# Four quadrants for the inverse's levels, and whole triangular blocks in seven transfers a half

## The chip, the core and the metric

The kernel runs on one core of one Trainium2 chip, in one launch. The metric is device time in microseconds of that core. TensorE (PE in the profile) does the matmuls and the transposes, VectorE (DVE) and ScalarE (ACT) the elementwise work, GpSimd (POOL) a few memsets, and the queue of SyncE (SP) issues every transfer, in the order in which the program has them. Each engine works through its own instructions in program order and waits where an operand is not there yet.

## The reference

One block of a hybrid model over 256 latent and 256 context tokens of width 2048: a modulated RMSNorm, one wide input projection, a bidirectional RWKV-7 branch of 16 heads, a latent-attention branch of 8 heads, gates, and an output projection. What the change touches is the recurrence of the RWKV branch, which runs over the context first and then over the latent tokens, in both directions `d`:

```python
def rwkv7_step(S, xs):
    r, w, k, v, kk, akk = xs
    sa = jnp.einsum("dbhij,dbhj->dbhi", S, -kk)
    S = S * w[..., None, :] + sa[..., :, None] * akk[..., None, :] + v[..., :, None] * k[..., None, :]
    return S, jnp.einsum("dbhij,dbhj->dbhi", S, r)
```

The kernel computes it in chunks of 64 tokens. Inside a chunk the terms `sa` depend on each other through a triangular 64x64 matrix A, so each chunk needs the inverse of a unit triangular matrix made from A.

## The kernel before, in words

All data are float32. Large products are done in three passes of split operands (`mm3`: high·high, high·low, low·high); each piece of weights `w` is loaded by SP, split into `wh` (ACT) and `wl` (DVE), and multiplied into an accumulator `acc`. Small products are plain float32 matmuls, and the profile has two records for each of these.

**Stages.** The norm, the modulation and the first projection take the start (to about 135 us). The RWKV stage follows (about 135 to 890 us): the 16 heads are 8 pairs, two heads of 64 channels on the two halves of the 128 partitions, and a pair has a context half (256 tokens) and a latent half, so there are 16 halves. Then come the attention branch and the merging products.

**The RWKV stage.** It is written as generators, which `drive` takes forward by an estimated clock. `front_chain` prepares halves (decays, keys, the triangular matrices `AQ`); `back_chain` takes groups: group 0 is the first pair's context half alone, groups 1 to 7 are the latent half of one pair beside the context half of the next, group 8 is the last latent half alone; `lanes` holds one generator `diagonal` for each half, one after the other; and where none of them is due, the planner puts in projection work (`bg`). The planner's waits in `diagonal` are the five numbers `LT`. They set only the order of the program, not a time on the chip. Each engine's instructions thus have a fixed order.

**The inverse of one half.** A half has 8 chunks-and-directions `u`, and 2 heads `g`, so 16 triangular 64x64 blocks. `diagonal` inverts the four 16x16 blocks on each diagonal: it writes them to DRAM (`dl`, 8 transfers), reads them back so that each of the 64 blocks of a `g`, `b` and `u` has a partition (`ln`, 1), inverts them by 28 small DVE steps and a few copies (`wt`, blocks and their transposes), writes them out (`dw`, 1), and reads them into the diagonal of `WT` (8), a tile of zeros otherwise: 18 transfers. There are two `WT`, one for context halves and one for latent halves; a new half is read into one once the `levels` of the group before are done.

**The levels.** `back` then finishes the inverses of a group in four steps, each with 16 matmuls of 64x64 by 64x64 for each half: first `Z` = the mask `zoff` times (`AQ`, `WT`), and then three times `W` = `WT` + (`Z` times `W`), where the first has `WT` in place of `W`. `lev` does one half's 16 matmuls: head 0 reads partitions 0 to 63 and writes PSUM partitions 0 to 63, head 1 reads 64 to 127 and writes 64 to 127. One DVE operation of 128x512 follows for each half (the mask, or the add of `WT`). After the levels the group goes through its four chunks (`chp` matmuls with `UV`, `xs`, `W`, `BKT`, `AR`, `QR`).

**The context half's products.** In `front` a context half's `AQ` comes from 8 matmuls of 128x128 by 128x128 with the block-diagonal tile `Qbd` (two heads, zeros between them); a latent half's from `QR`, by head, from 64 partitions each, in a burst (`E.burst`: after the first matmuls the rest of the group gets a high priority and is put behind them, so that nothing comes between).

In the profile, nearly all DVE and ACT instructions have the line of a helper (L141), and matmuls that of `Tensor.matmul` (L114, L116, L119); the names of the tiles tell them apart.

Of the kernel before, what the change touches and what calls it, by code (L numbers as in the profile page):

```python
# [16 lines left out]
P = 128  # L17
# [13 lines left out]
_CW = [("ident", 128), ("ones", 128), ("mq", 128), ("mr", 128),  # L31
# [29 lines left out]
LT = (3.0, 3.0, 2.0, 3.0, 4.0)  # L61
# [84 lines left out]
def hybrid_block(  # L146
# [128 lines left out]
    with tc.tile_pool(name="p1", bufs=2) as p1:  # L275
        xT = p1.tile([P, KT, TT], F32, name="xT", bufs=1)
# [47 lines left out]
        for k in range(KT):  # L324
# [6 lines left out]
            E.matmul(pst[32 * g:32 * g + 32], lhsT=con("ones")[:, 0:32], rhs=sq, start=k < 4, stop=k >= KT - 4,  # L331
# [4 lines left out]
        for i in range(4):  # L336
            E.matmul(pst[:, 2 * i:2 * i + 2], lhsT=sqs[:, 128 * i:128 * i + 128], rhs=con("ones")[:, 0:2], start=True, stop=True)
# [9 lines left out]
        E.matmul(pst, lhsT=con("ones"), rhs=dg.rearrange("p i t -> p (i t)"), start=True, stop=True)  # L347
# [244 lines left out]
    with tc.tile_pool(name="rw", bufs=1) as rw:  # L592
        WTs = []
        for i in range(2):
            WTs.append(rw.tile([P, 2, NU, CH], F32, name=f"WT{i}"))
            nc.gpsimd.memset(WTs[i], 0.0)


        Qbd = rw.tile([P, 2, 4, 2, CH], F32, name="Qbd")
        nc.gpsimd.memset(Qbd, 0.0)  # L600
# [10 lines left out]
        hss = [slice(0, 64), slice(64, 128)]  # L611
# [80 lines left out]
        def front(h, k, mi, rho):  # L692
# [67 lines left out]
            Q = rw.tile([P, 2, 4, 2, CH], F32, name="QR", bufs=2) if lat else Qbd  # L760
            ex = [slice(0, 64), slice(1, 65)]
            kkc = kk[:, ts].rearrange("p (c t) -> p c t", t=CH)
            for d in range(2):
                if lat:
                    V.scalar_tensor_tensor(Q[:, d, :, 0], kkc, -1.0, Ep3[d][:, :, ex[d]], ALU.mult, ALU.mult)
                else:
# [33 lines left out]
            else:  # L800
                for d in range(2):
                    ps = wk()
                    pv = ps.rearrange("p (c g t) -> p c g t", c=4, g=2)
                    for c in range(4):
                        E.matmul(pv[:, c], lhsT=BK[:, 4 * d + c].rearrange("p a t -> p (a t)"), rhs=Q[:, d, c], start=True, stop=True)
# [110 lines left out]
        def back(hs_, UV, rho):  # L916
# [695 lines left out]
```

## Time and profile before

| | |
|---|---|
| Time of 3 runs | 1264.83, 1268.13, 1276.66 us; median 1268.13 |
| The profiled execution's own time | 1267.55 us, of which its span is 1265.7 us |
| Granted TensorE clock, mean | 0.995 |
| Busy over the span | PE 1208.8, weight loads 1023.7, DVE 953.7, ACT 577.6, POOL 3.3 us |
| The RWKV stage, 200 to 890 us | PE 662.64, DVE 572.66, ACT 293.85 us busy of 690; DMA engines 0.42 |
| Matmuls of the levels (`lv`, 200 to 890 us) | 2048 records, PE 74.83 us |
| Transfers of a half's inverse | `dl` 8 of 8 KB, `ln` 64 KB, `dw` 128 KB, `WT` 8 of 16 KB |

A row of a timeline is: start, length, engine, line, operation, out<-in, shapes, count, and in brackets the idle time before it and what ended it. Matmuls overlap, and the length of one is its way through the array, so the pace of a sequence is read from the distances of the starts and not from the lengths. "x128" of the levels is 64 matmuls.

### The profile page before, as it was taken

Reading aid. Unit: us, or ns where it says so; the run is one execution under the profiler, and the core shown is the slowest. Engines: PE = TensorE matmul, PEld = TensorE weight load, DVE = VectorE, ACT = ScalarE, POOL = GpSimd, SP = SyncE. Lnnn points to the kernel's source line nnn. Section 1 sums busy time; section 2 is a strip of 40 time slices with the busy share of each in tenths; the row PEclk is TensorE's granted clock in tenths of the full one; section 3 lists DMA queues with packets and bytes.
Section 4 is the critical chain, followed back from the end, with each engine's and each line's share of the span. In section 5 each row is a group of like instructions: output and inputs, shape, how many; then the busy total and the mean of one; then the engine's idle time right before and its main releaser. Section 6 shows DMA issues by size and latency. Waiting matters only on the chain. (4 is left out here: it accounts for less than half of the span.)

```text
span 1265.7 us, 30073 instructions
## 1 busy us (share of the span) xinstructions
PE 1208.8 (96%) x11485; PEld 1023.7 (81%) x11485; DVE 953.7 (75%) x2658; ACT 577.6 (46%) x1216; POOL 3.3 (0%) x9
## 2 busy tenths in 40 slices
PE   6999999998999989999989999999999999899998
PEld 2566878787887877878778789889899999899886
DVE  4444777877898878888878988875876777768655
ACT  3444543442543434524524344444465656545443
POOL 0000000000000000000000000000000000000000
PEclk9999999999999999999999999999999999999999
DMA  9999345443442433443534345334765433589674
GB/s 377 347 358 335 130 146 165 145 125 115 125 131 78 135 91 106 138 113 92 152 98 118 107 132 155 108 102 136 249 197 159 131 115 115 185 275 304 217 256 140
DMA packets 170288, 212.10 MB, mean 168 GB/s; under 512 B 66512, under 2 KB 94816, under 8 KB 169632
## 3 DMA queue, kind: packets, MB, share of 16 engines
q1 hardware_dynamic: 170144, 210.18, 52.8%
q8 instruction: 90, 1.47, 0.5%
q14 instruction: 54, 0.44, 0.1%
HBM read 195.30 MB, written 14.82 MB: 166 GB/s over the span
## 5 line engine op out<-in xcount | busy, mean ns | idle before, releaser
L141 ACT CAST wh<-w 128x512 fp32r<-128x512 f32 (+1 forms) x484 | 290.9, 607 | 349.1 <-PE acc L119 142.8
L141 DVE TENSOR_TENSOR wl<-w,wh 128x512 fp32r<-128x512 f32 (+1 forms) x480 | 322.4, 674 | 144.8 <-ACT wh L141 73.7
L119 PE MATMUL acc<-hmh,wl 128*128 128x256 f32 (+1 forms) x1312 | 396.8, 302 | 5.2 <-DVE wl L141 4.5
L119 PE MATMUL acc<-hml,wh 128*128 128x256 f32 (+1 forms) x1312 | 393.5, 300 | 0.0
L119 PE MATMUL acc<-hmh,wh 128*128 128x256 f32 (+1 forms) x928 | 273.1, 294 | 0.0
L119 PEld LDWEIGHTS acc<-hmh,wl 128*128 128x128 f32 x1312 | 247.6, 189 | 20.6 <-DVE wl L141 9.2
L119 PEld LDWEIGHTS acc<-hml,wh 128*128 128x128 f32 x1312 | 248.2, 189 | 9.3 <-issue 1.0
L119 PEld LDWEIGHTS acc<-hmh,wh 128*128 128x128 f32 x928 | 175.4, 189 | 5.0
L116 PE MATMUL acc<-hmh,wh 128*128 128x256 f32 (+1 forms) x384 | 144.6, 377 | 6.5 <-DVE th L141 3.9
L116 PEld LDWEIGHTS acc<-hmh,wh 128*128 128x128 f32 x384 | 72.4, 189 | 32.0 <-issue 13.0
L141 DVE TENSOR_TENSOR pr<-wt 64x14 f32<-64x14 f32 (+6 forms) x224 | 42.7, 191 | 3.4
L141 DVE TENSOR_TENSOR wt<-wt,pr 64x14 f32<-64x14 f32 (+6 forms) x224 | 42.4, 189 | 3.3
L114 PE MATMUL a<-hmh,wh 128*128 128x512 f32 x96 | 40.7, 424 | 0.0
L114 PE MATMUL pm<-wm,ssil 128*32 128x256 f32 x512 | 35.0, 394 | 5.0 <-DMA wm<-in_w_mod_ss 4.9
L141 DVE TENSOR_TENSOR W<-WT,lv 128x512 f32<-128x512 f32 x48 | 32.2, 684 | 9.5 <-PE lv L114 9.5
L114 PE MATMUL a<-hmh,wl 128*128 128x512 f32 x96 | 38.0, 396 | 0.0
L114 PE MATMUL a<-hml,wh 128*128 128x512 f32 x96 | 37.9, 394 | 0.0
L114 PE MATMUL lv<-W,Z 64*64 64x64 f32 x1024 | 33.8, 220 | 3.9 <-DVE W L141 3.9
L114 PEld LDWEIGHTS lv<-W,Z 64*64 64x64 f32 x1024 | 31.7, 135 | 5.9 <-DVE W L141 5.1
L114 PE MATMUL chp<-obh,wh 128*128 128x256 f32 x128 | 36.2, 283 | 0.0
L114 PE MATMUL chp<-obh,wl 128*128 128x256 f32 x128 | 36.2, 283 | 0.0
L114 PE MATMUL chp<-obl,wh 128*128 128x256 f32 x128 | 36.2, 283 | 0.0
(327 smaller groups left out, 2166.3 us busy)
## 6 DMA issues: line engine op xcount, KB each, us to landing
w<-in_w_proj SPq DMA_DIRECT2D x296, 256.0 KB, 2.9
wm<-in_w_mod_ss SPq DMA_DIRECT2D x64, 512.0 KB, 7.2
w<-in_w_mod_g SPq DMA_DIRECT2D x64, 256.0 KB, 3.1
w<-in_w_br SPq DMA_DIRECT2D x64, 256.0 KB, 3.9
w<-in_w_out SPq DMA_DIRECT2D x64, 256.0 KB, 3.5
w<-in_w_first SPq DMA_DIRECT2D x32, 192.0 KB, 4.8
thd<-th SPq DMA_DIRECT2D x48, 128.0 KB, 2.9
xT<-in_xcT SPq DMA_DIRECT2D x4, 1024.0 KB, 8.4
```

Of the source, the lines that this page charges most:

```text
L114: return self.engine.matmul(out, lhsT=lhsT, rhs=rhs, **kw)
L116: self.head.append(self.engine.matmul(out, lhsT=lhsT, rhs=rhs, **kw))
L119: i = self.engine.matmul(out, lhsT=lhsT, rhs=rhs, **kw)
L141: return fn(out, *a, **kw)
```

## The change

The levels of a group with two halves are put into one burst, in which the matmuls of the two halves alternate; the latent half (member 0) stays on its partitions, and the context half (member 1) writes each result to the other 64 partitions than those that it reads, so that the four combinations of input and output halves come in turn. For this, `TF` is a copy of the context half's `WT` blocks with the partition halves exchanged, and `ZN` such a copy of its `Z` (four ACT copies of 64x512 for a group). Of its four steps, the first writes crossed, the next writes back, and so on.

`diagonal` moves whole 64x64 blocks: `dl` takes all of `AQ` (2 transfers), `ln` picks the diagonal blocks on its way from DRAM (1), `dw` puts the inverses on the diagonals of DRAM blocks that were filled with zeros once at the start (2, one for blocks and one for transposes), and `WT` is read whole (2): 7 transfers. `dw` is now one tile for each kind of half that stays, where a rotating tile was. `LT` is changed. The context half's products use a plain `Q` tile (`Qc`) and 16 matmuls with 64 partitions each, in a burst, in place of the 8 with `Qbd`. The constant `ones` of 128 columns is replaced by 2 columns and a memset tile in the two places that need more; `xs` shares a buffer with `ZN`.

```diff
-LT = (3.0, 3.0, 2.0, 3.0, 4.0)
+LT = (3.5, 5.0, 2.0, 4.5, 5.5)
+PD = CH * CH + CH
...
-            nc.gpsimd.memset(WTs[i], 0.0)
...
-        nc.gpsimd.memset(Qbd, 0.0)
+        WTs = [rw.tile([P, 2, NU, CH], F32, name=f"WT{i}") for i in range(2)]
+        nc.gpsimd.memset(WTs[0], 0.0)
+        dws = [dr1.tile([2, 8, 2, PD], F32, name=f"dw{i}") for i in range(2)]
+        for t in dws:
+            rows = t.rearrange("w u g (b x) -> (w u g b) x", b=4)
+            zero = WTs[0].rearrange("p w u t -> p (w u t)")
+            nc.sync.dma_start(rows[:, 0:16 * CH], zero)
+            nc.sync.dma_start(rows[:, 16 * CH:PD // 4], zero[:, 0:PD // 4 - 16 * CH])
...
-                    for g in range(2):
-                        hs = hss[g]
-                        V.scalar_tensor_tensor(Q[hs, d, :, g], kkc[hs], -1.0, Ep3[d][hs, :, ex[d]], ALU.mult, ALU.mult)
+                V.scalar_tensor_tensor(Q[:, d, :, 0], kkc, -1.0, Ep3[d][:, :, ex[d]], ALU.mult, ALU.mult)
...
-                    for c in range(4):
-                        E.matmul(pv[:, c], lhsT=BK[:, 4 * d + c].rearrange("p a t -> p (a t)"), rhs=Q[:, d, c], start=True, stop=True)
+                pv = [v4(wk()) for _ in range(2)]
+                with E.burst(tc, 2):
+                    for d in range(2):
+                        for c in range(4):
+                            for g in (1, 0):
+                                E.matmul(pv[g][:, d, c], lhsT=BK[hss[g], 4 * d + c].rearrange("p a t -> p (a t)"),
+                                         rhs=Q[hss[g], d, c, 0], start=True, stop=True)
...
+        def blocks(t):
+
+            return t.rearrange("u g (b x) -> (u g b) x", b=4)[:, 0:16 * CH].rearrange("p (r c) -> p r c", c=CH)[:, :, 0:16]
+
+        def diagonal(group, AQ, WT, dw):
+
+            dl = dram.tile([8, 2, PD], F32, name="dl", tag="dl")
             for g in range(2):
...
+                nc.sync.dma_start(dl[:, g, 0:CH * CH].rearrange("u (r c) -> r u c", c=CH), AQ[hss[g], g])
...
+            nc.sync.dma_start(ln, blocks(dl))
...
+            for w in range(2):
+                nc.sync.dma_start(blocks(dw[w]), wt[:, w])
...
+                nc.sync.dma_start(WT[hss[g]].rearrange("p w u t -> p (w u) t"),
+                                  dw[:, :, g, 0:CH * CH].rearrange("w u (r c) -> r (w u) c", c=CH))
...
-            def lev(fn):
-                ps = lvp()
-                for u in range(8):
-                    for g in range(2):
-                        fn(ps[hss[g], 64 * u:64 * u + 64], hss[g], g, u)
-                return v4(ps)
+            def lev(fns, outs, heads=n):
+                ps = [lvp() for _ in fns]
+                with E.burst(tc, heads):
+                    for u in range(8):
+                        for g in range(2):
+                            for t, fn, out in zip(ps, fns, outs):
+                                fn(t[hss[g ^ out], 64 * u:64 * u + 64], g, u)
+                return [v4(t) for t in ps]
...
+            def crossed(dst, src):
+
+                for g in range(2):
+                    S.copy(dst[hss[1 - g]], src[hss[g]])
...
+            if n == 2:
+                TF = rw.tile([P, 512], F32, name="TF")
+                crossed(v4(TF), top(WTs[0]))
+            ps = lev([lambda o, g, u, AQ=t[3], WT=WTs[t[1]]: E.matmul(o, lhsT=AQ[hss[g], g, u], rhs=WT[hss[g], 1 - u // 4, u], start=True, stop=True)
+                      for t in mem], (0, 1), 2 * n)
...
+            if n == 2:
+                ZN = rw.tile([P, 512], F32, name="ZN", tag="zx")
+                crossed(ZN, Zs[1])
...
+                for m in range(n):
+                    x = m * (1 - i % 2)
+                    Z = ZN if m and i == 1 else Zs[m]
+                    W = Ws[m] if i else TF if m else None
+                    fns.append(lambda o, g, u, Z=Z, W=W, x=x, WT=WTs[mem[m][1]]: E.matmul(
+                        o, lhsT=blk(Z, hss[g ^ x], u), rhs=WT[hss[g], u // 4, u] if W is None else blk(W, hss[g ^ x], u), start=True, stop=True))
+                ps = lev(fns, (0, i % 2))
+                for m in range(n):
+                    V.tensor_tensor(u4(W2[:, m]), v4(TF) if m and i == 1 else top(WTs[mem[m][1]]), ps[m], ALU.add)
```

**PE, the levels of group 4, before.** `WT_1358` is the context half's tile, `Z` and `W` the tiles of the levels, `QR` and `UV` belong to other steps:

```order
L114 MATMUL lv<-WT_1358,AQ 64x64 x15
L114 MATMUL chp<-UV,AQ 64x64 x4
L116 MATMUL wk<-QR,BK 128x128 x2
L119 MATMUL wk<-QR,BK 128x128 x6
L114 MATMUL lv<-WT_1358,Z 64x64 x16
L114 MATMUL lv<-W_6808,Z 64x64 x64
```

The last two steps of both halves stand in one row of 64 matmuls, half after half.

The same place now, from the end of the second step to the head of the third (`WT_1361` is the latent half's tile):

```order
L120 MATMUL lv<-WT_1361,Z 64x64
L120 MATMUL lv<-TF,Z 64x64
L117 MATMUL wk<-QR,BK 128x128 x2
L120 MATMUL wk<-QR,BK 128x128 x6
L117 MATMUL lv<-W_6863,Z 64x64
L117 MATMUL lv<-W_6863,ZN 64x64
```

The halves alternate matmul by matmul inside a step, and between two steps stands a piece of other work, here 8 products with `QR`; between the third and the fourth step there is a burst of `acc`.

**SP, the end of the second half's `diagonal`, before.** `dw` and `WT` are the two last transfers of the inverse, `w` are weights:

```order
L899 DMA dw<-wt 64x2x256
L236 DMA w<-in_w_proj 128x512
L906 DMA WT_1360<-dw 16x16x16 x8
L236 DMA w<-in_w_proj 128x512 x3
L236 DMA w<-in_w_mod_g 128x512 x2
```

And now, for the third half:

```order
L237 DMA w<-in_w_proj 128x512
L901 DMA dw_1363<-wt 64x16x16 x2
L905 DMA WT_1360<-dw_1363 64x16x64 x2
L237 DMA w<-in_w_proj 128x512 x3
L237 DMA w<-in_w_mod_g 128x512 x2
```

Nine transfers are four, and here no weights stand between the write and the read.

**SP, the start of the RWKV stage.** Now, the zero fill of both `dw` stands behind the first two pieces of the projection, where before 12 pieces followed each other:

```order
L707 DMA th<-in_wup 128x256
L237 DMA w<-in_w_mod_g 128x512 x2
L237 DMA w<-in_w_proj 128x512 x2
L603 DMA dw_1363<-WT_1360 128x1024
L604 DMA dw_1363<-WT_1360 128x16
L603 DMA dw_1364<-WT_1360 128x1024
L604 DMA dw_1364<-WT_1360 128x16
L237 DMA w<-in_w_proj 128x512 x10
```

Four transfers have moved in ahead of ten pieces of weights, and they read the tile that POOL sets to zero.

More of the change, by code (lines that the diff above doesn't have):

```diff
@@ L28 @@
 QK_SCALE = 192.0 ** -0.5
-_CW = [("ident", 128), ("ones", 128), ("mq", 128), ("mr", 128),
+_CW = [("ident", 128), ("ones", 2), ("mq", 128), ("mr", 128),
        ("zoff", 128), ("bones", 128), ("hsel", 2),
@@ L275, in hybrid_block @@
     with tc.tile_pool(name="p1", bufs=2) as p1:
+        ones = p1.tile([P, P], F32, name="ones", bufs=1)
+        nc.gpsimd.memset(ones, 1.0)
         xT = p1.tile([P, KT, TT], F32, name="xT", bufs=1)
@@ L330, in hybrid_block @@
             g = k % 4
-            E.matmul(pst[32 * g:32 * g + 32], lhsT=con("ones")[:, 0:32], rhs=sq, start=k < 4, stop=k >= KT - 4,
+            E.matmul(pst[32 * g:32 * g + 32], lhsT=ones[:, 0:32], rhs=sq, start=k < 4, stop=k >= KT - 4,
                      tile_position=(0, 32 * g))
@@ L336, in hybrid_block @@
         for i in range(4):
-            E.matmul(pst[:, 2 * i:2 * i + 2], lhsT=sqs[:, 128 * i:128 * i + 128], rhs=con("ones")[:, 0:2], start=True, stop=True)
+            E.matmul(pst[:, 2 * i:2 * i + 2], lhsT=sqs[:, 128 * i:128 * i + 128], rhs=con("ones"), start=True, stop=True)
         mod_a(0)
@@ L346, in hybrid_block @@
         V.tensor_tensor(dg, ident.unsqueeze(1).to_broadcast([P, 4, P]), rms[:, 0:8:2].unsqueeze(2).to_broadcast([P, 4, P]), ALU.mult)
-        E.matmul(pst, lhsT=con("ones"), rhs=dg.rearrange("p i t -> p (i t)"), start=True, stop=True)
+        E.matmul(pst, lhsT=ones, rhs=dg.rearrange("p i t -> p (i t)"), start=True, stop=True)
         rsb = p1.tile([P, TT], F32, name="rsb", bufs=1)
@@ L592, in hybrid_block @@
     with tc.tile_pool(name="rw", bufs=1) as rw:
[L593 to L599, printed above, removed]
-        nc.gpsimd.memset(Qbd, 0.0)
+        hss = [slice(0, 64), slice(64, 128)]
+        WTs = [rw.tile([P, 2, NU, CH], F32, name=f"WT{i}") for i in range(2)]
[6 more added lines that the diff above has]
+            nc.sync.dma_start(rows[:, 16 * CH:PD // 4], zero[:, 0:PD // 4 - 16 * CH])
         restart = rw.tile([P, 4 * 65], F32, name="restart")
@@ L934, in blk, with top @@
                 return t[hs, 64 * u:64 * u + 64]
+            def top(t):
+                return t.rearrange("p w (d c) t -> p (w d) c t", d=2)[:, 0:4:3]
+            def crossed(dst, src):
+                for g in range(2):
+                    S.copy(dst[hss[1 - g]], src[hss[g]])
             W2 = rw.tile([P, 2, 8, CH], F32, name="W2")
+            Ws = [W2[:, m].rearrange("p u t -> p (u t)") for m in range(n)]
             Zs = [t3("Z") for _ in mem]
-            ps = [lev(lambda o, hs, g, u: E.matmul(o, lhsT=AQ[hs, g, u], rhs=WTs[lat][hs, 1 - u // 4, u], start=True, stop=True))
-                  for p, lat, Q, AQ, AR, BKT in mem]
+            if n == 2:
[3 more added lines that the diff above has]
+                      for t in mem], (0, 1), 2 * n)
             for m in range(n):
                 V.tensor_tensor(v4(Zs[m]), ps[m], msk(zoff), ALU.mult)
+            if n == 2:
+                ZN = rw.tile([P, 512], F32, name="ZN", tag="zx")
+                crossed(ZN, Zs[1])
             yield
@@ L1160, in hybrid_block @@
         sin3 = gb[:, 192:256].rearrange("p (i h f) -> p i h f", i=2, h=2)
-        ones = con("ones")
+        ones = ml.tile([P, P], F32, name="ones", bufs=1)
+        nc.gpsimd.memset(ones, 1.0)
         def wk():
@@ L1503, in _constants @@
     c["ident"] = np.eye(P, dtype=f)
-    c["ones"] = np.ones((P, P), f)
+    c["ones"] = np.ones((P, 2), f)
     s = np.arange(CH)
```

42 lines of the change are left out of this document (7 added, 35 removed).

## The prediction, on record before the run

> **What bounds the kernel now.** I read the page's head first, then the busy times by stage, then PE's own waits, and last the timeline of one group's levels.
>
> ```profile
> span 1265.7 us, 30073 instructions
> PE 1208.8 (96%) x11485; PEld 1023.7 (81%) x11485; DVE 953.7 (75%) x2658; ACT 577.6 (46%) x1216; POOL 3.3 (0%) x9
> ```
>
> ```profile
> core 0: us, PE busy (x) PEld busy (x) DVE busy (x) ACT busy (x) POOL busy (x), PEclk, DMA share, GB/s
> 200.00:890.00 690.00, 662.64 (x7697) 564.12 (x7696) 572.66 (x1710) 293.85 (x650) 0.00 (x0) 1.00 0.42 120
> ```
>
> All that the change touches lies in the RWKV stage, and there PE stands idle for 690 − 662.64 = 27.4 us only, at full clock. DVE is next with 83%, ACT has 43%. Who ends PE's idle time (waits of that window, PE as engine):
>
> ```profile
> PE wk L116 <- DVE QR L141: 7.8, 5, 3.8
> PE chp L114 <- ACT UV L141: 4.9, 6, 2.5
> PE lv L114 <- DVE W L141: 3.9, 6, 1.0
> PE chp L114 <- DVE UV L141: 3.2, 7, 1.6
> PE acc L119 <- DVE wl L141: 2.4, 7, 0.8
> ```
>
> No row names a transfer. The planner always has projection work to put between the steps of the recurrence, so the stage is a queue of PE work, and what is taken out of that queue shortens it, as long as nothing new makes PE wait.
>
> **The levels.** Group 7 in the timeline of PE (start, length):
>
> ```profile
> 806.57 1.15 PE L114 MATMUL lv<-WT,Z 64*64 64x64 f32 x32
> 807.55 4.14 PE L114 MATMUL lv<-W,Z 64*64 64x64 f32 x128
> 811.62 0.45 PE L114 MATMUL chp<-UV,AQ 128*64 128x64 f32 x8
> ...
> 813.19 0.23 PE L114 MATMUL chp<-xs,W 64*64 64x64 f32 x2
> 813.21 0.22 PE L114 MATMUL chp<-QR,Mn 64*64 64x64 f32 x2
> 813.25 0.22 PE L114 MATMUL chp<-xs,W 64*64 64x64 f32 x2
> 813.26 0.23 PE L114 MATMUL chp<-QR,Mn 64*64 64x64 f32 x2
> 813.31 0.23 PE L114 MATMUL chp<-xs,W 64*64 64x64 f32 x2
> 813.32 0.23 PE L114 MATMUL chp<-QR,Mn 64*64 64x64 f32 x2
> 813.37 0.28 PE L114 MATMUL chp<-xs,W 64*64 64x64 f32 x4
> ```
>
> The 128 records of the last two steps start over about 4.14 − 0.22 = 3.92 us (0.22 is one matmul's length): 0.031 us a record, two records for each 0.061 us. There is no hole in it: while one half's add runs on DVE, PE works on the other half. The rows from 813.19 show the pace in four quadrants: `xs,W` stays on its partitions, `QR,Mn` writes to the other half, and four records start in each 0.06 us (813.19, 813.25, 813.31, 813.37). So a step of two halves, 64 records, takes 32 rounds of 0.06 now and 16 rounds then, which saves 0.96 us. Groups 1 to 7 have two halves and four steps each: **28 × 0.96 = 26.9 us less of PE work**. Groups 0 and 8 have one half and save nothing.
>
> The order differs from that of the rows at 813: there, every second pair of neighbours shares its input or output partitions, here every pair does. I take the full rate, and price the case against it as a rival.
>
> **New waits between the steps.** A step's burst now ends for both halves at once, and then two adds must run before the next one can start. DVE in the same place:
>
> ```profile
> 808.47 0.48 DVE L141 SCALAR_TENSOR_TENSOR kms<-cr,vv,kms 128x256 f32<-128x256 f32 x1
> 808.86 0.68 DVE L141 TENSOR_TENSOR W<-WT,lv 128x512 f32<-128x512 f32 x1
> 809.80 0.69 DVE L141 TENSOR_TENSOR W<-WT,lv 128x512 f32<-128x512 f32 x1 [0.26 <-PE lv L114]
> ```
>
> Two adds take some 1.3 us, with the last matmul's 0.22 and two hand-overs of about 0.05 together 1.6 us from the last matmul's start. What covers them is the work that the program puts between the steps. By the order that is mostly a burst of 12 `acc` (chain of waits, eleven behind the first, which itself takes about 0.2):
>
> ```profile
> 855.66 1.29 PE acc L119 x11
> ```
>
> That is 1.5 us, so 0.1 to 0.2 is left open. Only in groups 2 and 4 is the piece shorter: `UV,AQ` (8 records took 0.45 above) or eight products with `QR`, about 1.1 us; each leaves some 0.5 us. Of the 21 places between steps, 18 × 0.15 + 3 × 0.5 = 4 us. If DVE always takes the adds at once, 1 us; if each pair stands behind one more DVE operation of 0.7 us, 21 × 0.7 + 4 = 19 us. In the trace DVE waited for the matmuls at such places (0.26 above), so I take **+4**.
>
> The four crossing copies of a group, on ACT, have their nearest row in the copy of the same size:
>
> ```profile
> L141 ACT COPY AQ<-Qbd x8: 617/618/620, 206.7 to 804.4; 64x512 f32<-64x512 f32 x8
> ```
>
> 7 × 4 × 0.62 = 17 us of ACT, which is idle for 396 of the 690 us. `ZN` is needed two steps after its `Z`, 1.24 us of copying against at least one burst, two adds and a cover; `TF` one step after `WT` landed. I count both as covered; without cover the price would be 7 × 1.2 = 9 us.
>
> **The context half's products.** 8 matmuls of 128 weight columns by 128 become 16 of 128 by 64 on two row halves.
>
> ```profile
> 764.83 1.05 PE L114 MATMUL wk<-Qbd,BK 128*128 128x128 f32 x8
> 207.45 0.95 PE L114 MATMUL wk<-cc,sq 128*128 128x2 f32 x8
> 812.22 0.94 PE L119 MATMUL wk<-QR,BK 64*128 64x128 f32 x11
> ```
>
> Before, (1.05 − 0.27) / 7 = 0.11 us a record, 16 records, 1.8 us. The second row has only 2 columns and still takes (0.95 − 0.22) / 7 = 0.10: 128 weight columns set the pace, not the moved ones. The third is the latent half's form, at (0.94 − 0.27) / 10 = 0.067. 32 records at 0.067 are 2.1 us (8 × 0.3 = +3), at the 0.031 of the levels 1.0 us (8 × −0.8 = −6). The weights being what sets it, I take 0.06: **+1** in all. On DVE the half-sized products into `Qbd` halve in number (32 at 419 ns become 16 of the double width), 7 us off an engine that isn't the bound: 0.
>
> **Transfers.**
>
> ```profile
> L878 SPq DMA_DIRECT2D dl<-AQ x128: 303/429/1822, 167.9 to 821.0; - x128
> L906 SPq DMA_DIRECT2D WT<-dw x128: 303/447/1407, 198.2 to 844.3; - x128
> ...
> w<-in_w_proj SPq DMA_DIRECT2D x296, 256.0 KB, 2.9
> dl<-AQ SPq DMA_DIRECT2D x128, 8.0 KB, 1.6
> dw<-wt SPq DMA_DIRECT2D x16, 128.0 KB, 2.6
> WT<-dw SPq DMA_DIRECT2D x128, 16.0 KB, 2.1
> ln<-dl SPq DMA_DIRECT2D x16, 64.0 KB, 3.3
> ```
>
> 18 issues become 7: 11 × 0.44 × 16 = 77 us less of SP's queue, in which the weights stand behind them. PE's wait for split weights was 2.4 us there (above), 4.7 more at the weight loads' side, so the gain lies between 0 and 7: **−2**. In exchange each transfer is larger: `WT` 2 of 64 × 16 runs of 256 bytes, where 8 of 256 runs of 64 bytes were. A load of 256 KB in long runs lands after 2.9 us; going on from `dl` (128 runs, 1.6) and `WT` (256 runs, 2.1), 1024 runs would land after 2.1 + 768 × 0.004 = 5.1. Before, eight issues and a landing were 8 × 0.45 + 2.1 = 5.7 us, now 2 × 0.45 and 3 to 5, 4 to 6. The path is no longer than it was, and behind it stands the rest of the lane, for which the planner now leaves 20.5 us in place of 15: 0 for the forecast.
>
> **The start of the stage.** The zero fill waits for POOL and holds back the third piece of weights:
>
> ```profile
> 134.00 1.85 POOL L596 MEMSET WT<- 128x1024 f32 x2 [133.56 <-PE a L114]
> ...
> 135.98 1.28 SPq L236 DMA_DIRECT2D w<-in_w_proj  x3
> ...
> 138.52 0.62 ACT L141 CAST wh<-w 128x512 fp32r<-128x512 f32 x1 [0.21 <-DMA w<-in_w_proj]
> ```
>
> One memset ends at about 135.0, four issues of 0.4 follow, so the piece issued at 135.98 goes at 136.7, behind 1 MB of zeros. ACT already waits for that piece, so PE gets it 0.8 us later (the issue alone) to 4 us later (the zeros at the stage's best rate of some 300 GB/s): once, **+2.5**. The two new memsets of `ones` lie ahead of their use by transfers: 0.
>
> **The sum** against the profiled execution's 1267.55 us (the median of the runs, 1268.13, is 0.6 above it): 1267.55 − 26.9 + 4 + 1 − 2 + 2.5 = **1246**, 1.7% less.
>
> **The rivals.** (1) *The saving comes back as waits between the steps.* For it: DVE is 83% busy and serves the splits of the weights too, and the seamless alternation of the two halves is given up. Against it: DVE waited for PE at these places. It decides at 0.9 us for each of the 21 places, 19 us in all: 1246 + 19 = 1265, no change.
>
> (2) *Four quadrants don't start faster in this order.* PE would keep 0.031 us a record, and the sum without its first term is 1273, no change. The rows at 813 speak against it, neighbours with shared partitions for it. The Trainium skill (TensorE: Matmul & The Clock Gate, Part 1) has a rule of this kind: matmuls never start less than about 25 ns apart, however small. By that rule a step would still take 64 × 25 = 1.6 us, an estimate, and the time would be about 1263. The trace does not agree: rows of 813 start four records within 0.06 us, 15 ns each.
>
> (3) *Slower: the larger transfers land late.* PE takes its program in order, and the first matmuls of a group's levels stand in it where the planner thinks `WT` has landed; if it hasn't, all projection work behind them waits. For it: 2048 runs for each `WT`, four times the bytes, with the weights on the same queue. Against it: the shorter issue and the longer planned delay. It starts to cost more than the levels gain at (1268 − 1246) / 8 = 2.7 us of waiting ahead of each of 8 groups; with both halves' `WT` and `ln` late by 2 us each, 6 us for 6 of the groups, it is 1246 + 36 = 1282. The Trainium skill (DMA: Bandwidth & Descriptors, Specifications) speaks for this side: it wants 512 bytes or more for a transfer at line rate. The trace has only landings for runs of 64 bytes, 1.6 and 2.1 us, and shows no stall of PE on them; no run here has runs of 256 bytes.
>
> **How the numbers follow.** The forecast has 0.62, rival 1 0.15, rival 2 0.10, rival 3 0.07; 0.06 is for better than the sum, where SP's relief gives its 7 and the context products their 6 (1234). The forecast's own bounds are 1267.55 − 26.9 with waits 1 to 10, start 0.8 to 4, products −6 to +3 and SP 0 to −7: 1230 to 1258, the ends needing all at once. The range reaches from 1235 to 1268, where it takes in rival 1. A change of 1% is about what a measurement of this kernel can tell from none: faster needs less than 1255.5. Faster 0.64 (the forecast but for its upper edge, and the better case), same 0.28, slower 0.08.
>
> **What would show it.** Right: `lv` records at 15 ns in groups 1 to 7, the sum of `lv` busy time in the stage near 50 us in place of 74.8 (less would need single halves to gain too), PE idle in the stage under 35 us, the stage shorter by about 23 us and all others equal but for the first 3 us. Wrong: `PE lv <- DVE W` waits of 15 us or more (rival 1), `lv` records still 30 ns apart (rival 2), waits of PE or ACT on `WT<-dw`, or SP waiting long on `dw<-wt` (rival 3).

## The result, and the profile after

The changed kernel's ten runs lie between 1256.53 and 1264.17 us, median 1258.39; the kernel before, run beside it, has a median of 1271.7. The ratio is 0.9917, with a 95% interval of 0.9898 to 0.9936: 0.83% less time, where 1.7% was forecast. The time is inside the range, but half of the gain didn't come. The profiled execution took 1256.53 us, its span is 1254.7 us: 11.0 us under the one of before.

The levels first: all `lv` work of the stage (windows view: stretch, its length, busy time of PE, weight loads, DVE and ACT, then the granted clock, DMA share and GB/s), and the records of a step in group 5 (timeline of PE).

```profile
200.00:880.00 680.00, 50.25 (x2048) 41.83 (x2048) 41.96 (x64) 0.00 (x0) 1.00 0.53 138
```

```profile
634.10 0.27 PE L117 MATMUL lv<-WT,Z 64*64 64x64 f32 x1
...
634.26 0.22 PE L120 MATMUL lv<-WT,Z 64*64 64x64 f32 x1
634.27 0.22 PE L120 MATMUL lv<-TF,Z 64*64 64x64 f32 x1
634.28 0.22 PE L120 MATMUL lv<-WT,Z 64*64 64x64 f32 x1
634.28 0.22 PE L120 MATMUL lv<-TF,Z 64*64 64x64 f32 x1
634.32 0.22 PE L120 MATMUL lv<-WT,Z 64*64 64x64 f32 x1
```

Four records start in each 0.06 us, and 50.25 us stand where 74.83 stood: the levels give 24.6 us. The stage as a whole, from the first gate product to the last product with `AR`, before and then after:

```profile
135.30:881.20 745.90, 715.86 (x8051) 607.42 (x8052) 617.58 (x1829) 320.99 (x708) 1.79 (x4) 1.00 0.42 123
```

```profile
136.60:868.30 731.70, 695.31 (x8179) 583.90 (x8180) 601.16 (x1813) 339.61 (x736) 0.11 (x1) 0.99 0.53 139
```

It is 14.2 us shorter. PE's busy time fell by 20.5 us, so 4 of the 24.6 are taken back by other matmuls that run longer, and PE's idle time rose from 30.0 to 36.4 us. The stage also starts 1.3 us later, and what follows it takes 1.9 us more: −14.2 + 1.3 + 1.9 = −11.0.

PE's waits between 200 and 890 us (engine, line, what it waited for: sum, times, longest), to be held against the five rows shown of before:

```profile
PE lv L117 <- DVE W L142: 5.6, 11, 1.0
PE chp L115 <- DVE xs L142: 5.0, 4, 2.0
PE chp L115 <- DVE UV L142: 4.3, 7, 1.8
PE wk L117 <- DVE QR L142: 4.0, 5, 1.4
...
PE chp L115 <- DVE W L142: 1.7, 3, 1.2
PE lv L117 <- DVE Z L142: 1.3, 3, 0.6
```

Between two steps of the levels PE waited 5.6 + 1.3 = 6.9 us, before 3.9 for `W` and 0.2 for `Z`: +2.8. Ahead of the chunks' products with `xs` and `W` it waited 5.0 + 1.7 = 6.7 us, where before had this row alone:

```profile
PE chp L114 <- DVE xs L141: 1.4, 2, 0.9
```

That is +5.3, and the longest of these waits is there. Before, both waits of this row stand at later chunks of group 0, which has one half only. Now 0.8 us do, and the other 5.9 us stand at the first chunk behind the last step, in five of the seven groups with two halves: 2.0, 0.6, 1.1, 1.2 and 0.9 us in groups 1, 2, 4, 6 and 7. What DVE did ahead of the 2.03 us before `xs` in group 1, whose levels ended on PE at 307.4 (timelines of DVE and of PE):

```profile
309.70 0.43 DVE L142 TENSOR_TENSOR wal<-th,wah 128x256 fp32r<-128x256 f32 x1 [1.29 <-ACT wah L142]
...
311.07 0.67 DVE L142 TENSOR_TENSOR W<-WT,lv 128x512 f32<-128x512 f32 x1
311.67 0.20 DVE L142 TENSOR_TENSOR wt<-wt,pr 64x50 f32<-64x50 f32 x1
311.79 0.67 DVE L142 TENSOR_TENSOR W<-WT,lv 128x512 f32<-128x512 f32 x1
...
313.24 0.41 DVE L142 COPY xs<-chp 128x256 f32<-128x256 f32 x1
...
313.70 0.27 PE L115 MATMUL chp<-xs,W 64*64 64x64 f32 x2 [2.03 <-DVE xs L142]
```

The first add starts 3.7 us after the levels' last matmul has ended: DVE takes its instructions in order, and ahead of the add stand the small steps of the next half's block inverse (`pr`, `wt`) and an operation that waits for ACT. Then come the second add, a weight split and more small steps, and `xs` is last. In group 7, whose levels ended at 802.8, a transfer holds DVE up first:

```profile
804.03 0.66 DVE L142 COPY wt<-ln 32x256 f32<-32x256 f32 x2 [1.18 <-DMA ln<-dl]
...
805.46 0.67 DVE L142 TENSOR_TENSOR W<-WT,lv 128x512 f32<-128x512 f32 x1
...
807.55 0.41 DVE L142 COPY xs<-chp 128x256 f32<-128x256 f32 x1
...
808.02 0.27 PE L115 MATMUL chp<-xs,W 64*64 64x64 f32 x2 [0.94 <-DVE xs L142]
```

Waits on a transfer show on DVE, not on PE, and there is one more kind of place where PE pays for them:

```profile
479.38 0.66 DVE L142 COPY wt<-ln 32x256 f32<-32x256 f32 x2 [1.79 <-DMA ln<-dl]
...
480.79 0.63 PE L115 MATMUL chp<-UV,BKT 128*64 128x64 f32 x14 [1.77 <-DVE UV L142]
```

DVE stood at the head of a block inverse until `ln` had landed, the copy of the recurrence stood behind it, and PE behind that. Before has such waits too (`wt` on `ln` 8.6 us in sum there, 6.6 here). Their sum explains no difference of this pair, but here three of them, in groups 1, 4 and 7, stand ahead of the waits for `xs`.

The start of the stage: SP's fill and PE at the third piece of weights (timelines), then the stretch behind it (windows, granted clock third from the end).

```profile
136.36 0.33 SPq L603 DMA_DIRECT2D dw<-WT  x1
...
138.60 2.22 SPq L237 DMA_DIRECT2D w<-in_w_proj  x4
...
142.57 0.58 PE L117 MATMUL acc<-hmh,wh 128*128 128x256 f32 x1 [1.53 <-ACT wh L142]
```

```profile
142.00:149.20 7.20, 6.40 (x26) 6.00 (x27) 5.25 (x21) 3.19 (x6) 0.00 (x0) 0.53 0.56 183
```

The piece that went at 135.98 before goes at 138.60, PE waits 1.53 us, and then it runs for 6.83 us at half clock. That second part was in no term of the prediction.

### The profile page after: what moved, and what is told of

Its sections match the earlier page's. It is cut to its first block, busy times and chain, and to the rows that moved or that the text cites. A ratio compares the mean times of both kernels' runs of the same rounds, so it can differ in the third digit from the quotient of the medians.

```text
span 1254.7 us, 30101 instructions
## 1 busy us (share of the span) xinstructions
PE 1189.0 (95%) x11613; PEld 1000.5 (80%) x11613; DVE 937.7 (75%) x2642; ACT 596.4 (48%) x1244; POOL 1.9 (0%) x9
## 4 chain that ended last, share of the span: by engine, by line
PE 70%; DMA 15%; DVE 11%; issue 2%; ACT 2%; SPq 0%; DVEq 0%; ACTq 0%
PE acc L120 29%; PE chp L115 11%; PE lv L115 6%; PE acc L117 5%; DMA wm<-in_w_mod_ss 4%; PE a L115 4%; PE ch L115 3%; DMA w<-in_w_proj 3%; DVE wl L142 3%; PE wk L115 2%; PE wk L127 2%; DMA ln<-dl 2%; PE wk L120 2%; PE acc L115 1%; DVE wt L142 1%
## 5 line engine op out<-in xcount | busy, mean ns | idle before, releaser
L142 ACT ACTIVATE hx<-hx,mod 128x256 f32<-128x256 f32 x32 | 17.5, 594 | 37.8 <-DVE mod L142 37.8
L142 DVE TENSOR_TENSOR hml<-hx,hmh 128x512 fp32r<-128x512 f32 x16 | 11.1, 693 | 29.0 <-ACT hmh L142 29.0
L115 PEld LDWEIGHTS pm<-wm,ssil 128*32 128x32 f32 x512 | 13.4, 109 | 23.3 <-DMA wm<-in_w_mod_ss 11.5
```

The costliest lines, as they stand in the source:

```text
L115: return self.engine.matmul(out, lhsT=lhsT, rhs=rhs, **kw)
L142: return fn(out, *a, **kw)
```

## The experiments

All were timed in five rounds against the kernel before on the same chip. Beside the ratio I read three numbers. PE's idle time in the stage and, of it, the waits for the levels' own tiles (`W`, `Z`, `TF`, `ZN`, `xs`) are summed from the profiled execution; they count waits under 150 ns too, which the waits view leaves out (13.8 us for the changed kernel, where the view's rows add up to 13.6). The time lost to the clock is the span times one minus the mean granted clock, averaged over all timed executions (it counts a window at half clock also where PE stands idle in it); before has 7.1 to 8.6 us of it in the five sets, the changed kernel 13.3.

**First set: which part brings the time?** Theory A: the levels bring it, and what is missing went to the fill and the transfers. Theory B: waits between the joint steps eat half of it. Theory C: the transfers carry part of the gain.

The joint levels and the context products, with the old transfers, the old `LT` and no fill:

```diff
-LT = (3.5, 5.0, 2.0, 4.5, 5.5)
+LT = (3.0, 3.0, 2.0, 3.0, 4.0)
...
+                    nc.sync.dma_start(dl[:, 4 * g + b].rearrange("u r c -> r u c"), AQ[r0:r0 + 16, g, :, 16 * b:16 * b + 16])
...
+            nc.gpsimd.memset(WTs[i], 0.0)
...
```

> The changed kernel with the old 18 transfers, the old LT and no zero fill: the four-quadrant levels and the context half's new products stay. Theory A (the levels bring their PE time and little of it is lost at them; the missing part went to the zero fill at the start of the stage and to the transfers): 0.983 to 0.987 of the kernel before, 16 to 22 us less, better than the whole change (0.992). Theory B (the waits between the joint steps eat half of it, the transfers cost nothing): 0.990 to 0.993, the same as the whole change. Theory C (the seven transfers relieve the queue and carry part of the gain): 0.994 or more.

Measured: 1277.55 us, ratio 1.006 (1.0038 to 1.0083): slower than before, although PE's levels are nearly as short as in the changed kernel (51.7 us from start to start, 47.0 there, 71.6 before). PE idles 43.2 us in the stage, and 26.3 us are lost to the clock. The worst place, in the windows view (granted clock third from the end), and DVE and PE there:

```profile
721.01:724.42 3.41, 0.07 (x1) 0.00 (x0) 1.50 (x6) 0.17 (x1) 0.00 (x0) 1.00 0.33 120
724.42:731.25 6.83, 5.83 (x60) 5.49 (x62) 4.34 (x16) 0.81 (x2) 0.00 (x0) 0.50 0.15 38
```

```profile
722.88 0.66 DVE L142 COPY wt<-ln 32x256 f32<-32x256 f32 x2 [1.99 <-DMA ln<-dl]
...
725.42 0.37 PE L115 MATMUL chp<-xs,W 64*64 64x64 f32 x2 [4.34 <-DVE xs L142]
```

DVE waits for `ln`, the adds and `xs` stand behind it in its order, PE stands for 4.34 us and then has half its clock for 6.83 us. A falls: the levels alone bring nothing in this order of the program.

Everything but the joint levels:

```diff
-                with E.burst(tc, heads):
-                    for u in range(8):
-                        for g in range(2):
-                            for t, fn, out in zip(ps, fns, outs):
-                                fn(t[hss[g ^ out], 64 * u:64 * u + 64], g, u)
+                for u in range(8):
+                    for g in range(2):
+                        fn(ps[hss[g], 64 * u:64 * u + 64], hss[g], g, u)
...
```

> The changed kernel with the levels as before (half after half, two quadrants, no burst, no crossing copies): the seven transfers, LT, the zero fill and the context products stay. Theory A: 1.003 to 1.006 of the kernel before (4 to 8 us more, from the start of the stage). Theory B: 0.999 to 1.001. Theory C: 0.994 to 0.998.

Measured: 1266.37 us, ratio 0.9984 (0.9966 to 1.0002). PE idles 21.7 us, 2.2 of it for the levels' tiles; 10.0 us are lost to the clock. So the transfers and the products alone bring 0.16%, and nothing at all is still inside the interval. Against this kernel the joint levels take 25.3 us from PE and add 14.7 us of idle time.

The changed kernel, with the fill issued behind the first read `ln`:

```diff
...
+            fill()
...
```

> The whole change, but the zero fill of both DRAM tiles is issued behind the first half's read of its diagonal blocks, some 30 us into the stage, and not ahead of the third piece of weights. Theory A: 3 to 6 us less than the whole change, 0.987 to 0.989 of the kernel before, and no idle time of PE of 1.5 us with a half clock behind it near 141 us. Theories B and C: within 1 us of the whole change, 0.991 to 0.993.

Measured: 1256.4 us, ratio 0.9897 (0.9861 to 0.9934), span of the profile 1251.4 against 1254.7. The fill costs about 3 us by the spans of one profiled execution each, and the half clock at the stage's start is gone; the intervals of the two ratios overlap.

The kernel before with the new context products alone:

```diff
-                        E.matmul(pv[:, c], lhsT=BK[:, 4 * d + c].rearrange("p a t -> p (a t)"), rhs=Q[:, d, c], start=True, stop=True)
+                                E.matmul(pv[g][:, d, c], lhsT=BK[hss[g], 4 * d + c].rearrange("p a t -> p (a t)"),
+                                         rhs=Q[hss[g], d, c, 0], start=True, stop=True)
...
```

> The kernel before with the context half's products in 16 matmuls of 128 columns by 64 on two row halves from the plain tile, nothing else changed. If 128 weight columns set the pace of a record: 0.999 to 1.002. If the moved columns did, 32 records at 0.031 us: 6 us less, 0.995.

Measured: 1268.57 us, ratio 0.9989 (0.9966 to 1.0011). The records start in pairs, one for each half of the partitions, and a pair comes every 0.11 us, as one record of the old form did: half the moved columns don't shorten it.

**Second set: the planned waits.** The kernel of ratio 1.006 and the changed kernel differ in the transfers, the fill and `LT`. Theory D: what counts is when DVE reaches the transfers' data; theory E: the transfers themselves.

```diff
-LT = (3.0, 3.0, 2.0, 3.0, 4.0)
+LT = (3.5, 5.0, 2.0, 4.5, 5.5)
```

> The joint levels and the context products with the 18 old transfers, as in the run that gave 1.006, but with the changed kernel's planned waits LT (3.5, 5, 2, 4.5, 5.5). Theory D (the order): what made that run slow is that DVE, which works in order, reached the first step of a block inverse (wt<-ln) before ln had landed, 11.6 us in all, with the copies UV and xs of the recurrence queued behind it, and PE behind those; the read is now planned 2 us later, so DVE waits on ln for under 6 us, PE's gaps above 1 us fall from seven to two or three, and the ratio to the kernel before is 0.990 to 0.995. Theory E (the transfers): eight issues for dl and eight for WT are themselves what is late; the waits on ln stay near 10 us and the ratio at 1.00 to 1.01.

Measured: 1264.24 us, ratio 0.9945 (0.9925 to 0.9966). D's ratio came, but not its reason: DVE's waits on `ln` rose from 11.6 to 14.9 us. What changed is that PE no longer stands for so long at once (2.3 us at most, 4.3 there): 13.4 us are lost to the clock in place of 26.3. Span times mean clock is 1248.9 us in this kernel and 1248.8 in that one: the whole difference is the clock. The changed kernel has the same `LT` and the new transfers with their fill; it is 0.3% lower, and the intervals overlap.

The changed kernel with the old `LT`, the reverse edit:

> The changed kernel with the planned waits LT of before (3, 3, 2, 3, 4). Theory D (the order): DVE waits on ln for 10 us or more instead of 6.6, PE's idle time in the stage rises by 5 to 10 us, ratio to the kernel before 0.995 to 1.003. Theory E (the transfers): with two issues in place of eight the data are there in time in any case; idle as in the changed kernel, ratio 0.988 to 0.994.

Measured: 1271.02 us, ratio 1.0006 (0.9991 to 1.0021): the whole gain is gone with five numbers that only set the order. PE's idle time is as in the changed kernel, 36.8 us; 20.7 us are lost to the clock. D's detail was wrong here too (DVE's waits on `ln` are 7.2 us). With the old waits of the planner the levels meet their data late, the transfer `WT` among them (waits of PE):

```profile
PE lv L117 <- DMA WT<-dw: 3.5, 3, 2.1
```

And a step of joint levels at half clock, to compare with the rows at 634 (two starts 0.11 us apart in place of 0.06):

```profile
698.54 0.31 PE L120 MATMUL lv<-WT,Z 64*64 64x64 f32 x1
...
698.65 0.31 PE L120 MATMUL lv<-WT,Z 64*64 64x64 f32 x1
```

The late fill, with the adds and `xs` given priority on DVE:

```diff
...
+                with tc.high_priority(HB):
+                    V.tensor_copy(xs[:, 0:n], dt(px[:, 0:128 * n]))
```

> The changed kernel with the late zero fill, and the adds W of the levels and the copy xs given the highest priority on DVE, so that less stands ahead of them in its order. Theory D: PE's waits for xs and W (some 9 us in gaps above half a us) fall to 4 or less, the half-clock window at 308 us goes, ratio 0.984 to 0.987 to the kernel before. Rival F (DVE is simply full: whoever is first, another is later): those waits fall, but waits for wl, QR or UV rise by as much, ratio 0.988 to 0.991.

Measured: 1255.89 us, ratio 0.9885 (0.986 to 0.991). PE's waits for `xs` are gone, those for `W` are 6.8 us, for `UV` 6.3, for `wl` 4.2; idle 35.2 where 34.6 was. The rival is right: the waits moved.

The late fill, with the first step of the block inverse planned 3 us later behind its read:

```diff
-LT = (3.5, 5.0, 2.0, 4.5, 5.5)
+LT = (3.5, 8.0, 2.0, 4.5, 5.5)
```

> The changed kernel with the late zero fill and the planned wait between the read ln and the first step of the block inverse at 8 instead of 5. Theory D: DVE's waits on ln fall from 6.5 to under 2 us, and with them PE's gaps behind UV and xs near 477 and 557 us (3 us), ratio 0.985 to 0.988. Rival G: the inverse then ends later, WT lands later than the levels are planned, and PE waits on WT<-dw instead; or the order changes elsewhere by as much: ratio 0.990 or more.

Measured: 1262.63 us, ratio 0.9937 (0.9921 to 0.9952). DVE still waits 5.9 us on `ln`, idle 39.8 us. The rival holds.

**Third set: is DVE's queue the bound?** First `xs` on ACT, with the late fill:

```diff
-                V.tensor_copy(xs[:, 0:n], dt(px[:, 0:128 * n]))
+                S.copy(xs[:, 0:n], dt(px[:, 0:128 * n]))
```

> The changed kernel with the late zero fill and the copies xs (four a group) on ACT in place of DVE. Theory D, in the form that the last runs left of it (DVE's queue is where the levels' gain is lost: the two adds of a step, the copies of the recurrence, the weights' wl and the block inverse share it): 0.41 us a copy leaves DVE, PE's waits for xs (5.7 us) fall to 2 or less, PE's idle time in the stage from 34.6 to about 29, ratio to the kernel before 0.983 to 0.987. Rival (ACT's own queue is as long: xs then waits behind wh, UV and the crossing copies): PE waits for ACT rise by as much, ratio 0.989 to 0.993.

Measured: 1268.2 us, ratio 0.9984 (0.9963 to 1.0005), worse than either expectation. `xs` waits 2.7 us for ACT, but idle is 37.9 and 15.2 us are lost to the clock.

Then the 28 steps of each block inverse left out, in the changed kernel and in the one before:

```diff
...
-                    V.tensor_tensor(pr[:, 0:k, 0:m], X[:, 0:k, k:k + 1].to_broadcast([64, k, m]),
-                                    X[:, k, k + 1:16].unsqueeze(1).to_broadcast([64, k, m]), ALU.mult)
-                    V.tensor_tensor(X[:, 0:k, k + 1:16], X[:, 0:k, k + 1:16], pr[:, 0:k, 0:m], ALU.add)
+                    for _ in range(2):
+                        clock.ready = V.t = max(V.t, clock.ready) + k * m / V.rate + V.fixed
```

> The changed kernel without the 28 small DVE steps of each block inverse (the blocks are copied as they are; the planner's clock counts the steps as before). Theory D: DVE loses 16 times about 5 us, 80 us, and what PE waits for DVE falls with it: idle time in the stage from 36.4 to 22 or less, the half-clock windows in the stage from three to one or none, ratio to the kernel before 0.976 to 0.984. Rival (the waits between the joint steps come from the adds and the hand-overs themselves, not from what else stands in DVE's queue): the waits for W, xs and UV stay at 12 us or more, ratio 0.988 to 0.992.

> The kernel before without the same 28 steps of each block inverse. Theory D: its levels alternate half by half and leave room for DVE, so it gains less than the changed kernel does by the same cut: ratio 0.992 to 0.998, against 0.8 to 1.5 per cent there. Rival: DVE's steps cost both kernels alike, ratio 0.985 to 0.990 here, and the distance between the two kernels stays 0.8 per cent.

Measured: 1260.03 us, ratio 0.9931 (0.9908 to 0.9954) for the changed kernel, and 1265.22 us, 0.9972 (0.9954 to 0.9991) for the one before. Without these steps neither kernel computes the right inverse; they are timed to see what DVE's load costs. With some 50 us less of DVE in the stage the changed kernel is no faster than with it. Idle is 33.4 us; the waits for the levels' tiles fell to 6.2, but now PE waits for weights (first two rows of the waits view):

```profile
PE acc L117 <- ACT wh L142: 8.1, 6, 3.3
PE acc L120 <- DVE wl L142: 3.4, 8, 0.9
```

Idle is 20.9 us in the kernel before without the steps, so 12.5 us still lie between the two. As far as theory D blames DVE's load it has fallen. Its order is another matter: in this kernel too the first add or mask of a joint step starts 1.6 us on average after the step's last matmul has ended, against 1.1 in the changed kernel.

The changed kernel without the crossing copies:

```diff
-                    Z = ZN if m and i == 1 else Zs[m]
-                    W = Ws[m] if i else TF if m else None
+                    Z = Zs[m]
+                    W = Ws[m] if i else None
...
```

> The changed kernel without the crossing copies TF and ZN (four ACT copies a group); their places take the uncrossed tiles, so that the matmuls keep their partitions and their order but multiply other blocks. As predicted (the copies are covered): 17 us less of ACT, PE unchanged, ratio to the kernel before 0.990 to 0.994. Rival (they are not covered: 1.2 us a group): idle time falls by 5 to 9 us, ratio 0.984 to 0.988.

Measured: 1262.84 us, ratio 0.9943 (0.992 to 0.9965), idle 39.8. The matmuls then multiply other blocks, so the result is not the function any more. Taking the copies away brought nothing, so they are covered; that the ratio is 0.3% higher, with overlapping intervals, is no more than what another order does here.

**Fourth set: more cover.** Theory I: the work between two joint steps is too short.

```diff
...
-                yield
+                yield 1.0 if n == 2 else None
```

> The changed kernel with 1.0 more in the planner's wait behind each of the four steps of a group's joint levels, so that more projection work stands in PE's order between them. Theory I (thin cover: PE waits because the work between two joint steps is as short as the two adds, and the clock falls because single waits are over 1.4 us): PE's waits for W and Z at lv and chp (8.6 us in the changed kernel) fall to 3 or less, idle time in the stage from 36.4 to 28 or less, the time lost to the clock (span times one minus the mean granted clock, 13.3 us there) to 10 or less, ratio to the kernel before 0.980 to 0.987. Rival (whatever is put there is taken from another place, and each group's chain gets 3 us longer): idle stays at 33 or more, ratio 0.990 to 0.996.

Measured: 1266.2 us, ratio 0.9963 (0.9947 to 0.998). The waits for the levels' tiles fell from 13.8 to 7.5 us, and idle is 37.9: those for `wh`, `rvb` and others took their place.

Half of that with the late fill, and then `LF` in place of it:

> The changed kernel with the late zero fill and 0.5 more in the planner's wait behind each step of the joint levels. Theory I: between the late fill alone and the full cover, W and Z waits 5 us or less, ratio 0.982 to 0.988. Rival: another order with other waits, ratio 0.988 to 0.995.

```diff
-LF = 0.4
+LF = 0.7
```

> The changed kernel with the late zero fill and the share LF of the planned engine time that the planner waits behind every step of the recurrence at 0.7 in place of 0.4: cover for the chunk steps too. Theory I: PE's waits for W, xs and UV together (15 us in the late fill kernel) fall to 7 or less, lost clock time 8 us or less, ratio 0.980 to 0.986. Rival (the recurrence's chain gets too long for the projection work that is left: a tail without filler at the end of the stage): stage longer, ratio above 0.992.

Measured: 1268.64 us, ratio 0.9982 (0.9967 to 0.9997), idle 44.8; and 1266.04 us, ratio 0.9973 (0.9958 to 0.9988), idle 31.5 with 21.4 us lost to the clock, in a stage that is 46 us longer, as the rival said. I falls.

**Fifth set: the two adds.** Theory J: both adds of 128x512 stand between two steps; split in halves, they can start while PE still works on the step.

```diff
...
-                for m in range(n):
-                    V.tensor_tensor(u4(W2[:, m]), v4(TF) if m and i == 1 else top(WTs[mem[m][1]]), ps[m], ALU.add)
+                for d in ([slice(0, 1), slice(1, 2)] if n == 2 else [slice(0, 2)]):
+                    for m in range(n):
+                        T0 = v4(TF) if m and i == 1 else top(WTs[mem[m][1]])
+                        V.tensor_tensor(u4(W2[:, m])[:, d], T0[:, d], ps[m][:, d], ALU.add)
```

> The changed kernel with the late zero fill, in which each mask and each add of a group with two halves is done in two operations of 128x256: first both halves' first four blocks, then both halves' last four. So the adds of the first blocks can run while PE works on the last ones, and the next step can start behind two short adds (0.8 us) in place of two long ones (1.3 us after the step's end). Theory J (the price of the joint steps is that both adds stand between two steps): PE's waits for W, Z and xs in the stage, which are 11 us on average in the kernels with joint levels, fall to 6 or less, idle to 30 or less, ratio to the kernel before 0.982 to 0.987. Rival (56 more DVE operations and another order cost as much as is gained): waits for W, Z and xs as before, ratio 0.988 to 0.996.

> The same split of the masks and adds in the changed kernel itself, whose fill stands at the start: the same edit in a second order of the program. Theory J: ratio 0.984 to 0.989, waits for W, Z and xs 6 us or less. Rival: 0.990 to 0.998, waits as before.

Measured: 1262.13 us, ratio 0.9936 (0.9916 to 0.9957), and 1267.1 us, 0.9973 (0.9954 to 0.9993). The waits for the levels' tiles fell, 12.9 to 8.2 and 13.8 to 6.8 us, and idle rose, 34.6 to 43.3 and 36.4 to 40.9: the rival holds for the time. In the first of the two, these rows have come up:

```profile
PE wk L117 <- DVE QR L142: 5.3, 5, 1.7
PE lv L117 <- DVE wt L142: 5.0, 2, 2.9
```

**What all of them show together.** Means over the kernels of each kind, each kernel counted once:

| | 4 without joint levels | 15 with them |
|---|---|---|
| PE in the levels, start to start, us | 72.1 (71.2 to 73.3) | 48.5 (44.7 to 51.7) |
| PE idle in the stage, us | 23.6 (20.9 to 30.0) | 38.3 (31.5 to 44.8) |
| of it for the levels' tiles and `xs`, us | 2.9 (1.3 to 5.5) | 10.3 (6.2 to 16.7) |
| span times mean clock, us | 1256.7 (1254.8 to 1260) | 1247.1 (1242.0 to 1252.4) |
| lost to the clock, us | 8.7 (6.7 to 10.4) | 15.5 (9.4 to 26.3) |
| ratio to the kernel before | 0.997 to 1 | 0.9885 to 1.006 |

On average over these orders the joint levels take about 24 us from PE, give some 15 back as idle time, and then lose 7 us more to the clock. That leaves 3 us. Some of these orders were expected to be worse, but the changed kernel's 11 us are clearly not what the matmuls bring in any order. Where the idle time falls can be moved from one tile to another, but none of nine edits aimed at it, or at what feeds it, brought it under 31 us. Only the late fill, alone or with the priority, has a ratio below the changed kernel's, and by less than their intervals; no version clearly beats it.

## Why the prediction was half right

| term | forecast | the profiled pair |
|---|---|---|
| levels, PE | −26.9 | −24.6 |
| waits for the levels' tiles | +4 | +8.1: between the steps +2.75, behind the last +5.86, at group 0's later chunks −0.53 |
| context products | +1 | −0.2 |
| SP's relief | −2 | −1.7 (waits for weights, without that of 1.53 at the start) |
| start of the stage | +2.5 | +1.5: a wait of 1.53 |
| work ahead of the stage | 0 | +1.3 |
| all other PE work and waits | 0 | other PE work +4.2, other waits −1.5 |
| behind the stage | 0 | +1.9 |

**The levels** were right in mechanism and nearly in size: 15 ns a record. The missing 2.3 us lie partly at the head of each step, where the first records start 0.10 us before the next four (634.10, 634.21) and not 0.06.

The 1.3 us ahead of the stage are not the fill's: with nearly the same program up to there, the stage starts between 133.4 and 136.7 us in 18 of the 19 traces, with the early fill and without it. And SP's relief is near its term by luck rather than shown: no run isolates it, and behind 200 us only 0.4 of the 1.7 are found.

**The step that failed** is "In the trace DVE waited for the matmuls at such places", from which +4 takes the two adds to run at once. In the 28 joint steps of the changed kernel the first of the two adds or masks starts 1.06 us on average after the step's last matmul has ended, and more than 0.3 us after it in 18 of them; the second starts after 1.7. Before, the last add or mask of a step started 0.44 us after its matmuls, and 0.05 behind each of the seven last steps. For the 21 places between the steps the sum still came out (+2.8 for +4), but by luck: PE has 2.4 us of other work there on average, not the 1.5 of one burst. And "of the 21 places between steps" leaves out the seven places behind the fourth step. There both adds must be done before the first chunk's products with `W`, and the copy `xs` follows on the same DVE. Before, PE waited at none of them; now it waits 5.9 us at five, more than the +2.8 of the other 21, although in groups 1, 4 and 7 two bursts of `acc` stand there as cover: DVE comes late to the adds or to `xs`, behind `ln`, the block inverse and the weights' splits. The premise behind it, that what is taken out of PE's queue shortens the stage "as long as nothing new makes PE wait", was right; that the planner "always has" work to put in between was read from a program whose order had been matched to halves in turn.

**What no term had** is the clock. All timed executions together show it: span times mean clock fell by 16 us, from 1260 (the kernel before in the five sets) to 1243.9, and the loss to the clock rose by 5 to 6, from 7.1 to 8.6 up to 13.3. The prediction took "at full clock" from the stage's mean of 1.00 and held it fixed. Of the +4.2 in other PE work 1.7 is this (10.2 us at half clock in the stage, before 6.8, half of the difference); the rest is spread over the 2,792 `acc` records, and I did not follow it.

**Rival 1**, the saving coming back as waits, was the nearest: not at 0.9 us in each place, but in part, and at places it had not named. (Its 1265 adds 19 us to a sum that has +4 of them already; with the +4 taken out it is 1261.) **Rival 2** fell with the rows at 634. The Trainium skill's floor of about 25 ns between starts (TensorE: Matmul & The Clock Gate, Part 1) doesn't hold over four quadrants: 15 ns here. **Rival 3** fell for this kernel: no row of PE names `WT<-dw`, although the larger reads land near the upper end of the 3 to 5 us that I had put (before: 16 KB, 2.1):

```profile
WT<-dw SPq DMA_DIRECT2D x32, 256.0 KB, 4.8
```

With the old `LT` it does appear, at 3.5 us. So the longer planned wait was needed, and it is the changed kernel's order, as much as its matmuls, that keeps the gain: with the old numbers it is 1.0006.

**What stays open.** Why the idle time stays near 38 us whatever is moved isn't settled. That the adds of a joint step come late in DVE's order is seen in every kernel with joint steps and whole adds (0.8 to 1.6 us on average for the first), also without the block inverse; that this is the cause, and that any planned order then misses somewhere by 1 or 2 us, fits all runs but was not shown by one. The waits of DVE for `ln` are a rival for a part of it: no run has the joint steps without them, but the run with the least of them (3.1 us, the split adds in the changed kernel) idles 40.9 us. That a wait is followed by half clock was seen in every trace, but no run made waits of a set length to test it.

## What to carry to other kernels

Where two independent chains are merged into one for a faster matmul rate, count every hand-over that one chain hid for the other, the one behind the last step too, and look in the other engine's order for what stands ahead of it there. On PE a wait has two prices, its length and the clock behind it: before trusting a sum of busy times, look for single waits of some 1.5 us or more and add half of the windows that follow. And where five planning numbers move the time by 0.9%, a change of half a per cent must be tried in more than one order before it is put down to the mechanism.

## What the runs showed of the hardware

The granted clock is 1.00 or 0.50, in windows of 3.41 us on a grid that runs through the whole execution. Over the 19 traces of this case, full-speed windows between 150 and 900 us, sorted by how long PE was idle in them:

| PE idle in a window of 3.41 us | next window at full clock | at half clock |
|---|---|---|
| under 0.75 us | 3744 | 3 |
| 0.75 to 1.5 | 224 | 20 |
| 1.5 to 1.75 | 11 | 16 |
| 1.75 to 2 | 2 | 21 |
| 2 and more | 0 | 16 |

So some 1.5 us of waiting within one window are enough, and a wait that straddles two windows can go free. One wait of 1.9 us behind the first group's levels (for `rnb`) stands in most kernels. In the changed kernel the grid cuts it, 0.50 us in one window and 1.36 in the next, and the clock stays; in the changed kernel with the old `LT` it lies in one window, and the next one has half clock:

```profile
213.96:217.37 3.41, 2.05 (x39) 1.75 (x40) 3.18 (x10) 1.09 (x3) 0.00 (x0) 1.00 0.14 52
```

```profile
209.00:212.41 3.41, 1.46 (x34) 1.33 (x35) 2.65 (x14) 1.96 (x4) 0.00 (x0) 1.00 0.92 228
212.41:215.82 3.41, 3.41 (x42) 2.85 (x43) 1.63 (x4) 0.00 (x0) 0.00 (x0) 0.50 0.05 19
```

The grid lies differently in each execution, and that fits, though no run shows it, the scatter between runs of one kernel: the changed kernel's run at a mean clock of 0.993 took 1256.53 us, the one at 0.986 took 1264.17. The Trainium skill (TensorE: Matmul & The Clock Gate, Part 1) describes this window, free-running and 3.4 us long, and the traces agree; it warns of idle gaps over 3.4 us, and here the measured bound is less than half of that.
